# Attention products over 128 rows only, the second dilated group in whole segments of 256 keys, and rotary tables in each group's token order

## The chip, the cores and the metric

The kernel runs on one core of a Trainium2 chip. The metric is the device time of one execution in microseconds, median of several runs; smaller is better. Engines are named as the profile names them: PE is TensorE (its weight loads are PEld), DVE is VectorE, ACT is ScalarE, POOL is GpSimd, and SP is SyncE, whose queue issues most DMAs.

## The reference, cut to what matters

Two layers over 1024 tokens of 1024 channels. Each layer projects the normed input into four token mixers and their gates. The change lies in the third mixer, attention in three groups of four heads of 64 channels. Group 0 attends over neighbouring tokens, group 1 over every fourth and group 2 over every sixteenth, each within 64 places to either side:

```python
DILATED_CFG = ((128, 1), (512, 4), (2048, 16))
...
q = apply_rope(qkv[:, :, 0], cos, sin)
k = apply_rope(qkv[:, :, 1], cos, sin)
for g, (window, dil) in enumerate(DILATED_CFG):
    o, l = dilated_window_attention(q[:, :, g], k[:, :, g], v[:, :, g], dil, window // (2 * dil))
...
valid = (jnp.abs(qi - kj) <= half) & (kj >= 0) & (kj < L)
s = jnp.where(valid, s, NEG_BIG)
```

The group's order of tokens puts those of one residue side by side: one stretch of 1024 tokens in group 0, four of 256 in group 1, sixteen of 64 in group 2. Outputs of the groups are mixed by the softmax of their log-sum-exps.

## The kernel before, in words

Everything is float32, computed from pairs of shorter numbers: each operand is split into hi and lo (`split`: ACT copies hi, DVE subtracts lo), and a product takes three passes, hi by hi, hi by lo, lo by hi. Channels lie on partitions, tokens along the free axis, in halves of 512.

The main line of PE is one projection after another: `in_unit` loads 512 KB of weights, splits them and runs 24 products (L128, z) for each half of the tokens; `evac` empties the sum. Side work is written as generators in lanes; after every second group of passes `tick` lets each lane take a step, so that tiles of attention ("att"), taps of the convolution ("taps", 240 DVE instructions of L841), and the rest stand between the main products. The scheduler of the tile framework then fixes one order for each engine, and each engine works through its own in that order.

In each layer there are two pairs of heads, and for each pair the three groups. `att_group` runs the units of q, k and v of a group; then `att_tiles` of that group runs as side work during the units of the next.

`rope_unit` empties each half of a q or k unit. ACT copies the sums out of PSUM (rt, L365), four DMAs of 64 KB turn 32 rows at a time (rot, L367 and L368), three DVE instructions apply the tables, which lie in natural order of the tokens, and then come the split copies: these read rot in the group's order (a stride of 4 or 16 in groups 1 and 2) and write qa, qb, ka, kb in that order. A tile holds for head a hi above lo and for head b lo above hi. For q it is hi twice (L375, L377, four ACT copies), and lo of both heads in a third tile ql (L383 on ACT, L384 on DVE).

`products` makes the scores of two tiles of 128 queries: for each head one product over 128 rows (hi of q by hi and lo of k, L457) and one over 64 rows (lo of q by hi of k, L460), where those of the two heads use different halves of the array. `scores` adds the mask and takes the maximum on DVE, then the exponential on ACT (p, L474). `transposed` turns p on PE (pt, L486) and splits it; `weighted` multiplies by v (pv, L128) and ACT copies it out (o, L517). In groups 0 and 1 a tile's window begins 64 keys before it, so v lies in tiles of 64 rows at a segment's edges (veh, vel) and of 128 rows within it (vfh, vfl). A segment of group 1 has 256 keys and two tiles of queries, each with a window of 192 keys: one piece of 64 and one of 128.

Places for large tiles come from pools by tag: A has 11 (q, k and o among others), M has 11 (v's tiles, cos and sin among others).

Of the kernel before, what the change touches and what calls it, by code (L numbers as in the profile page):

```python
# [14 lines left out]
P = 128  # L15
# [23 lines left out]
# columns of the packed per-layer parameters  # L39
C_G, C_CW, C_CB, C_LG, C_LB, C_PS, C_BG, C_N = 0, 8, 70, 72, 74, 76, 78, 110  # L40
# columns of the packed constants
K_ID, K_M, K_M2, K_BC, K_BS, K_ED, K_IS, K_SG, K_O2, K_N = (
    0, 128, 384, 512, 640, 768, 800, 802, 804, 806)


class Net:
# [41 lines left out]
    def half_pair(self, name, tag):  # L88
        """hi and lo of one [P, H] operand."""
        t = self.slot(name, F32R, tag=tag)  # L90
        return t[:, 0:H], t[:, H:S]
# [10 lines left out]
    def split(self, hi, lo, src):  # L102
        """hi + lo = src exactly, each part with few enough bits for one pass."""
        self.nc.scalar.activation(out=hi, in_=src, func=AF.Copy)  # L104
        self.nc.vector.tensor_tensor(out=lo, in0=src, in1=hi.bitcast(F32), op=ALU.subtract)  # L105

    def load_unit(self, src, kc=KC, n=P, tag=None, ahead=AHEAD):
        """A right shape of weights: hi and lo."""
# [24 lines left out]
    def gemm(self, ps, w, x, hf, main=True):  # L133
        """x[k][hf]: hi and lo of the k-th 128 rows of the right operand, one half of the tokens."""
        self.passes(ps, [((w[0][:, k], w[1][:, k]), xk[hf]) for k, xk in enumerate(x)], main)

# [1 line left out]
    def setup(self):  # L138
# [4 lines left out]
        self.mask = c[:, K_M:K_M + 256]  # L143
# [9 lines left out]
    def load_constants(self):  # L153
        dma = self.nc.sync.dma_start
        dma(out=self.c, in_=self.a["consts"])
# [12 lines left out]
    def tok_stat(self, chunks, ones, name):  # L168
        """PSUM [token, 4 tiles, 2]: the mean over channels of the given [P, H] chunks' columns."""
# [24 lines left out]
    def spread(self, st, name):  # L194
        """[token, 4 tiles] to PSUM [P, H], the same in every partition."""
# [53 lines left out]
    def together(self, ws, xs, pss, ks=range(KC)):  # L249
        """Products that share their right operands."""  # L250
# [79 lines left out]
    def first_units(self, l, units):  # L330
        """Their first halves of the tokens before the second ones, whose norm is still under way."""
# [8 lines left out]
    def perm_dst(self, ap, g, hf):  # L340
        """Where the tokens of half hf lie in group g's order."""
# [4 lines left out]
        return ap.rearrange("p (r n) -> p r n", r=r)[:, :, hf * n:(hf + 1) * n]  # L346

# [5 lines left out]
    def rope_unit(self, l, u, g, cos, sin, q):  # L353
        """The rotated unit, split and stacked, for each of the two heads (a: rows 0:64, b: rows 64:128).
        For k: hi over lo (a), lo over hi (b). For q: hi twice (a, b), and lo, both heads."""
# [3 lines left out]
        xl = self.slot("ql", F32R) if q else None  # L359
        top, bot = slice(0, 64), slice(64, P)  # L360

        def evac(hf, ps):
            sl = slice(hf * H, hf * H + H)
            t, r = self.t2("rt"), self.t2("rot")
            nc.scalar.activation(out=t, in_=ps, func=AF.Copy)  # L365
# [3 lines left out]
            nc.vector.tensor_tensor(out=t, in0=t, in1=cos[:, sl], op=ALU.mult)  # L369
            nc.vector.tensor_tensor(out=r, in0=r, in1=sin[:, sl], op=ALU.mult)  # L370
            nc.vector.tensor_tensor(out=r, in0=r, in1=t, op=ALU.add)
            dst = lambda x, rows: self.perm_dst(x, g, hf)[rows]
            src = lambda rows: self.perm_src(r, g)[rows]
            for x, own, other in ((xa, top, bot), (xb, bot, top)):
                nc.scalar.activation(out=dst(x, own), in_=src(own), func=AF.Copy)  # L375
                if q:
                    nc.scalar.activation(out=dst(x, other), in_=src(own), func=AF.Copy)  # L377
                else:
                    nc.vector.tensor_tensor(out=dst(x, other), in0=src(own), in1=dst(x, own).bitcast(F32),
                                            op=ALU.subtract)  # L380
            if q:
                al = slice(0, P)
                nc.scalar.activation(out=dst(xl, al), in_=src(al), func=AF.Copy)  # L383
                nc.vector.tensor_tensor(out=dst(xl, al), in0=src(al), in1=dst(xl, al).bitcast(F32), op=ALU.subtract)  # L384
        self.in_unit(l, u, evac)
        return (xa, xb, xl) if q else (xa, xb)
# [9 lines left out]
    def v_tiles(self, vt, g, where):  # L396
        """v in the group's token order, tokens on partitions: hi, lo, rows by key offset."""
# [3 lines left out]
        if g == 2:  # L401
# [20 lines left out]
    def att_group(self, l, hp, g, cos, sin, done):  # L422
# [5 lines left out]
    def att_tiles(self, l, hp, g, q, k, vt, done):  # L428
# [7 lines left out]
        def window(t):  # L436
# [4 lines left out]
            a, b = max(base, q0 - 64), min(base + L, q0 + 192)  # L441
            m0 = a - (q0 - 64)
            return a, [a, q0 + 64], self.mask[:, m0:m0 + b - a]
# [3 lines left out]
        def products(t):  # L447
            # one bank per head: the two heads' products run in different rows of the array
            b = [self.aux("s0"), self.aux("s1")]
            s = {}  # L450
            for i in range(2):
# [4 lines left out]
                for h in range(2):  # L456
                    mm(s[i][h], q[h][:, qs], k[h][:, a:a + n], start=True, stop=False)  # L457
                for h in range(2):
                    r = slice(64 * h, 64 * h + 64)
# [805 lines left out]
```

## Time and profile before

| what | before |
|---|---|
| runs, median (lowest to highest) | 2097.05 us (2096.38 to 2097.84) |
| the profiled execution, span | 2096.5 us |
| PE busy | 2023.1 us (96%) |
| DVE busy | 1487.6 us (71%) |
| ACT busy | 1100.2 us (52%) |
| mean granted clock of PE | 0.985 |
| DMA, mean | 123 GB/s |

The page gives the profiled execution no time of its own beside the span. Busy time is an average over stages; PE is at or near full outside of the two attention stages (from about 110 to 450 us, and from 1170 to 1445 us). A row of the timeline reads: start in us, length in us, engine, line, operation, output<-input, shape, and in brackets how long the engine had stood idle and what ended that.

### The profile page before, as it was taken

What the parts mean: (1) busy time and instruction counts of PE and PEld (TensorE: products, weight loads), DVE (VectorE), ACT (ScalarE), POOL (GpSimd) and SP (SyncE); (2) the same over time, 40 slices, a digit from 0 to 9 for tenths busy, and PEclk for the clock granted to TensorE, in tenths of its full rate; (3) what the DMA queues carried; (4) which work ended last, traced back from release to release, by engine and by line L of the source; (5) the groups of instructions that cost most, each with busy time, mean ns of one, the idle gap of its engine ahead of it and who ended that gap; (6) DMA issues with size and microseconds to landing.
All of it is one profiled execution on the core that took longest, in us unless ns stands there. A gap on an engine that the chain in (4) does not pass through costs nothing.

```text
span 2096.5 us, 26763 instructions
## 1 busy us (share of the span) xinstructions
PE 2023.1 (96%) x9500; PEld 1645.9 (79%) x9500; DVE 1487.6 (71%) x2752; ACT 1100.2 (52%) x2025; POOL 41.3 (2%) x90
## 2 busy tenths in 40 slices
PE   8998898999999999999999998989999999999998
PEld 6776686778878888887888776867888888888888
DVE  7596777775657877877655867687555867777775
ACT  7347666657755433434321566666685744344451
POOL 0000000000000000000000000000000000000000
PEclk9999998999999999999999999999999999999999
DMA  6231122212586234236421321223127843243443
GB/s 229 81 106 58 49 82 62 96 41 81 190 284 235 86 136 141 100 112 245 158 85 49 106 65 52 77 71 101 46 87 266 278 159 125 97 141 131 144 167 101
DMA packets 122438, 257.81 MB, mean 123 GB/s; under 512 B 31808, under 2 KB 36544, under 8 KB 122304
## 3 DMA queue, kind: packets, MB, share of 16 engines
q1 hardware_dynamic: 111360, 216.25, 31.1%
q0 software_dynamic: 10944, 39.85, 5.6%
q8 instruction: 75, 1.23, 0.2%
q14 instruction: 59, 0.48, 0.1%
HBM read 176.16 MB, written 67.30 MB: 116 GB/s over the span
## 4 chain that ended last, share of the span: by engine, by line
PE 73%; DVE 10%; ACT 9%; DMA 4%; issue 3%; SPq 1%; DVEq 0%; ACTq 0%
PE z L128 20%; PE ga L128 12%; PE g L128 8%; PE gb L128 8%; PE py L128 8%; PE op L128 6%; PE z L255 3%; DVE cv L841 2%; PE pv L128 2%; PE pt L486 1%; ACT p L474 1%; DVE w L105 1%; ACT qa L377 1%; ACT ql L383 1%; ACT qb L375 1%
## 5 line engine op out<-in xcount | busy, mean ns | idle before, releaser
L128 PE MATMUL z<-h,w 128*128 128x512 f32 x3000 | 760.9, 404 | 1.4 <-DVE gp L604 1.4
L128 PEld LDWEIGHTS z<-h,w 128*128 128x128 f32 x3000 | 557.0, 192 | 119.5 <-DVE gp L604 1.8
L104 ACT ACTIVATE w<-wr 128x1024 fp32r<-128x1024 f32 (+1 forms) x135 | 137.8, 1022 | 185.9 <-PE z L128 80.2
L105 DVE TENSOR_TENSOR w<-wr,w 128x1024 fp32r<-128x1024 f32 (+1 forms) x135 | 158.9, 1179 | 97.8 <-ACT w L104 81.6
L128 PE MATMUL ga<-t,wf 128*128 128x512 f32 x768 | 188.9, 395 | 0.0
L128 PE MATMUL gb<-t,wf 128*128 128x512 f32 x768 | 187.4, 393 | 0.0
L128 PE MATMUL g<-h,wf 128*128 128x512 f32 x768 | 186.3, 391 | 0.0
L128 PE MATMUL op<-m,w 128*128 128x512 f32 (+1 forms) x960 | 181.3, 349 | 2.0 <-DVE m L105 1.9
L128 PE MATMUL py<-g,w 128*128 128x512 f32 x768 | 181.5, 395 | 0.5 <-ACT y L930 0.5
L841 DVE SCALAR_TENSOR_TENSOR cv<-cv,params 128x512 f32<-128x512 f32 x240 | 178.9, 745 | 2.2
L128 PEld LDWEIGHTS op<-m,w 128*128 128x128 f32 x960 | 153.6, 189 | 28.0 <-DVE m L105 3.5
L128 PEld LDWEIGHTS ga<-t,wf 128*128 128x128 f32 x768 | 144.3, 188 | 33.6
L128 PEld LDWEIGHTS py<-g,w 128*128 128x128 f32 x768 | 143.3, 188 | 34.3 <-ACT y L930 1.7
L128 PEld LDWEIGHTS gb<-t,wf 128*128 128x128 f32 x768 | 144.3, 188 | 32.9
L128 PEld LDWEIGHTS g<-h,wf 128*128 128x128 f32 x768 | 144.2, 188 | 31.9
L104 ACT ACTIVATE wf<-wr 128x512 fp32r<-128x512 f32 x144 | 90.9, 632 | 130.4 <-issue 48.4
L105 DVE TENSOR_TENSOR wf<-wr,wf 128x512 fp32r<-128x512 f32 x144 | 98.8, 686 | 21.5 <-ACT wf L104 20.3
L474 ACT ACTIVATE p<-p,nm 128x192 f32<-128x192 f32 (+2 forms) x192 | 84.4, 441 | 54.0 <-DVE nm L471 53.6
L105 DVE TENSOR_TENSOR pl<-pt,ph 128x256 fp32r<-128x256 f32 (+2 forms) x136 | 63.2, 465 | 54.1 <-ACT ph L104 53.8
L104 ACT ACTIVATE wf<-s 128x512 fp32r<-128x512 f32 x64 | 40.4, 632 | 107.3 <-PE gb L128 64.4
L128 PE MATMUL ga<-h,wf 128*128 128x512 f32 x384 | 93.5, 392 | 0.0
L128 PEld LDWEIGHTS ga<-h,wf 128*128 128x128 f32 x384 | 72.1, 188 | 16.4
(246 smaller groups left out, 2832.4 us busy)
## 6 DMA issues: line engine op xcount, KB each, us to landing
wr<-in_w_in_dram SPq DMA_DIRECT2D x75, 512.0 KB, 3.7
y<-y SPq DMA_DIRECT2D x128, 256.0 KB, 3.8
y<-y POOLq DMA_DIRECT2D x64, 512.0 KB, 4.8
wr<-in_w_gate_dram SPq DMA_DIRECT2D x48, 512.0 KB, 4.4
wr<-in_w_out_dram SPq DMA_DIRECT2D x32, 512.0 KB, 3.6
rot<-rt SPq DMA_DIRECT2D x192, 64.0 KB, 2.0
cv<-in_w_gate_dram SPq DMA_DIRECT2D x16, 512.0 KB, 5.1
wr<-in_w_branch_dram SPq DMA_DIRECT2D x16, 512.0 KB, 5.0
```

What stands on the lines that cost most here:

```text
L104: self.nc.scalar.activation(out=hi, in_=src, func=AF.Copy)
L105: self.nc.vector.tensor_tensor(out=lo, in0=src, in1=hi.bitcast(F32), op=ALU.subtract)
L128: self.nc.tensor.matmul(ps, w, x, start=(first and i + u == 0), stop=(i == n - 1 and u == 2), skip_group_check=open_)
L255: self.nc.tensor.matmul(ps, a[:, k], b, start=(k + j == 0), stop=(k == KC - 1 and j == 2))
L375: nc.scalar.activation(out=dst(x, own), in_=src(own), func=AF.Copy)
L377: nc.scalar.activation(out=dst(x, other), in_=src(own), func=AF.Copy)
L383: nc.scalar.activation(out=dst(xl, al), in_=src(al), func=AF.Copy)
L474: nc.scalar.activation(out=ph, in_=ph, func=AF.Exp, bias=nm[:, h:h + 1], accum_out=st[:, t, 2 + h:3 + h])
L486: nc.tensor.transpose(pt[:rows[ci], cs], p[:, off:off + rows[ci]], self.ident)
L841: self.tc.keep_in_program_order(nc.vector.scalar_tensor_tensor(out=y, in0=u[:, j:j + H], scalar=tap(j), in1=y, op0=ALU.mult, op1=ALU.add))
```

## The change

`rope_unit` now empties PSUM in the group's order at once: the ACT copy rt reads the sums with the stride and writes them side by side, and the DMAs, the tables and the split copies all work in that order. So the tables lie in DRAM three times, once for each group's order, and `att_group` loads cos and sin for each group of each head pair (24 loads of 512 KB in place of 4).

q is split like k: qa holds hi above lo, qb lo above hi (two ACT copies and two DVE subtractions per half). Once both halves are there, four DMAs of 256 KB copy the halves of the rows crosswise into two new tiles qt. `products` then takes for each head two products over all 128 rows: qa by ka gives hi by hi plus lo by lo, qt by ka gives the cross terms. lo by lo was not computed before. A group holds four tiles for q in place of three.

In group 1 every tile of queries now takes the whole segment of 256 keys, as two pieces of 128; the mask grows from 256 to 384 columns, and v is turned in eight tiles of 128 rows with none of 64. The Fourier basis (256 columns) leaves the constants and is loaded by `fourier_pq`.

```diff
     def rope_unit(self, l, u, g, cos, sin, q):
         xa, xb = self.slot(name + "a", F32R), self.slot(name + "b", F32R)
-        xl = self.slot("ql", F32R) if q else None
+        turned = [self.slot("qt", F32R) for _ in range(2)] if q else []
         def evac(hf, ps):
-            t, r = self.t2("rt"), self.t2("rot")
-            nc.scalar.activation(out=t, in_=ps, func=AF.Copy)
+            t, r, rc = self.t2("rt"), self.t2("rot"), self.t2("rc")
+            nc.scalar.activation(out=self.in_order(t, g), in_=self.perm_src(ps, g), func=AF.Copy)
...
-            src = lambda rows: self.perm_src(r, g)[rows]
+            src = lambda rows: self.in_order(r, g)[rows]
             for x, own, other in ((xa, top, bot), (xb, bot, top)):
                 nc.scalar.activation(out=dst(x, own), in_=src(own), func=AF.Copy)
-                if q:
-                    nc.scalar.activation(out=dst(x, other), in_=src(own), func=AF.Copy)
-                else:
-                    nc.vector.tensor_tensor(out=dst(x, other), in0=src(own), in1=dst(x, own).bitcast(F32),
-                                            op=ALU.subtract)
-            if q:
-                al = slice(0, P)
-                nc.scalar.activation(out=dst(xl, al), in_=src(al), func=AF.Copy)
-                nc.vector.tensor_tensor(out=dst(xl, al), in0=src(al), in1=dst(xl, al).bitcast(F32), op=ALU.subtract)
+                nc.vector.tensor_tensor(out=dst(x, other), in0=src(own), in1=dst(x, own).bitcast(F32),
+                                        op=ALU.subtract)
+            if hf == 1:
+                for x, y in zip((xa, xb), turned):
+                    for to, of in ((top, bot), (bot, top)):
+                        nc.sync.dma_start(out=y[to].bitcast(F32), in_=x[of].bitcast(F32))
         self.in_unit(l, u, evac)
-        return (xa, xb, xl) if q else (xa, xb)
+        return (xa, xb, *turned)

     def v_tiles(self, vt, g, where):
-        if g == 2:
+        if g:
             full = [j * P for j in range(8)]

+    def in_order(self, ap, g):
+        return ap if g == 0 else ap.rearrange("p (r n) -> p r n", r=4 if g == 1 else 16)

-    def att_group(self, l, hp, g, cos, sin, done):
+    def att_group(self, l, hp, g, done):
+        cos, sin = self.slot("cos", tag="M"), self.slot("sin", tag="M")
+        for i, t in enumerate((cos, sin)):
+            self.nc.sync.dma_start(out=t, in_=self.a["rope"][g, i])

         def window(t):
-            a, b = max(base, q0 - 64), min(base + L, q0 + 192)
-            m0 = a - (q0 - 64)
-            return a, [a, q0 + 64], self.mask[:, m0:m0 + b - a]
+            if g == 1:
+                a, b = base, base + L
+            else:
+                a, b = max(base, q0 - 64), min(base + L, q0 + 192)
+            m0 = a - q0 + P
+            return a, [a, a + P if g == 1 else q0 + 64], self.mask[:, m0:m0 + b - a]

         def products(t):
                 for h in range(2):
-                    mm(s[i][h], q[h][:, qs], k[h][:, a:a + n], start=True, stop=False)
-                for h in range(2):
-                    r = slice(64 * h, 64 * h + 64)
-                    mm(s[i][h], q[2][r, qs], k[h][r, a:a + n], start=False, stop=True)
+                    for j in (0, 2):
+                        mm(s[i][h], q[h + j][:, qs], k[h][:, a:a + n], start=(j == 0), stop=(j == 2))

     def fourier_pq(self, l, us, res):
+        bcs = self.t2("bcs")[:, 0:2 * P]
+        nc.sync.dma_start(out=bcs, in_=self.a["consts"][:, K_BC:K_ALL])

 def _constants():
+    rope = np.stack([rope.reshape(2, P, 2, H // r, r).transpose(0, 1, 2, 4, 3).reshape(2, P, S) for r in (1, 4, 16)])
```

How the instructions stand now is shown at three places in the first layer's first head pair, where group 1's tiles run beside group 2's units. On PE, the first pair of score tiles of group 1 (s0 and s1 are the sums of the two heads); before:

```order
L457 MATMUL s0_1876<-ka_1341,qa_1196 128x192
L457 MATMUL s1_1877<-kb_1342,qb_1197 128x192
L460 MATMUL s0_1876<-ka_1341,ql_1198 128x192
L460 MATMUL s1_1877<-kb_1342,ql_1198 128x192
L457 MATMUL s0_1876<-ka_1341,qa_1196 128x192
L457 MATMUL s1_1877<-kb_1342,qb_1197 128x192
L460 MATMUL s0_1876<-ka_1341,ql_1198 128x192
L460 MATMUL s1_1877<-kb_1342,ql_1198 128x192
```

and of the change:

```order
L465 MATMUL s0_1881<-ka_1353,qa_1205 128x256
L465 MATMUL s0_1881<-ka_1353,qt_1207 128x256
L465 MATMUL s1_1882<-kb_1354,qb_1206 128x256
L465 MATMUL s1_1882<-kb_1354,qt_1208 128x256
L465 MATMUL s0_1881<-ka_1353,qa_1205 128x256
L465 MATMUL s0_1881<-ka_1353,qt_1207 128x256
L465 MATMUL s1_1882<-kb_1354,qb_1206 128x256
L465 MATMUL s1_1882<-kb_1354,qt_1208 128x256
```

The eight products stay eight; those with ql, over 64 rows, are replaced by products with qt over 128 rows, a head's two follow each other, and the columns go from 192 to 256.

On ACT, the second half of group 2's q unit (rot_1813 before, rot_1831 now) and the first exponentials of group 1 (p with st1); before:

```order
L375 ACTIVATE qa_1682<-rot_1813 64x16x32
L377 ACTIVATE qa_1682<-rot_1813 64x16x32
L375 ACTIVATE qb_1683<-rot_1813 64x16x32
L377 ACTIVATE qb_1683<-rot_1813 64x16x32
L383 ACTIVATE ql_1684<-rot_1813 128x16x32
L365 ACTIVATE rt_1906<-z_1836 128x512
L474 ACTIVATE p_1886,st1_1875<-p_1886,nm_1887 128x192 x2
L474 ACTIVATE p_1893,st1_1875<-p_1893,nm_1894 128x192 x2
```

and of the change:

```order
L370 ACTIVATE rt_1918<-z_1857 128x512
L380 ACTIVATE qa_1700<-rot_1831 64x16x32
L380 ACTIVATE qb_1701<-rot_1831 64x16x32
L479 ACTIVATE p_1891,st1_1880<-p_1891,nm_1892 128x256 x2
L479 ACTIVATE p_1898,st1_1880<-p_1898,nm_1899 128x256 x2
```

Two copies stand ahead of the exponentials where five stood, and k's copy out of PSUM has moved ahead of both.

On SP's queue, the rotations of group 2's q (second half, rot_1831) and k (rot_1919, rot_1995) in the changed kernel:

```order
L373 DMA rot_1831<-rt_1830 32x512
L372 DMA rot_1919<-rt_1918 32x512
L386 DMA qt_1702<-qa_1700 64x1024 x2
L386 DMA qt_1703<-qb_1701 64x1024 x2
L373 DMA rot_1919<-rt_1918 32x512
L372 DMA rot_1919<-rt_1918 32x512
L373 DMA rot_1919<-rt_1918 32x512
L372 DMA rot_1995<-rt_1994 32x512
L373 DMA rot_1995<-rt_1994 32x512
L372 DMA rot_1995<-rt_1994 32x512
L373 DMA rot_1995<-rt_1994 32x512
L427 DMA cos_2185<-in_rope_dram 128x1024
```

The four copies into qt stand within the rotation of k's first half, each waiting for qa or qb to be written; before, nothing stood between q's rotations and k's but a weight load. The next group's tables follow, and wait until earlier tiles of v give up their places.

In ACT's order the first write of kb now waits, in nine of the ten groups that follow another in their layer, for the last score products of the group before, whose q or k tile had its place; before, only the copies qb and ql of one group in each layer waited for such products.

More of the change, by code (lines that the diff above doesn't have):

```diff
@@ L40 @@
 C_G, C_CW, C_CB, C_LG, C_LB, C_PS, C_BG, C_N = 0, 8, 70, 72, 74, 76, 78, 110
-K_ID, K_M, K_M2, K_BC, K_BS, K_ED, K_IS, K_SG, K_O2, K_N = (
-    0, 128, 384, 512, 640, 768, 800, 802, 804, 806)
+K_ID, K_M, K_M2, K_ED, K_IS, K_SG, K_O2, K_N, K_BC, K_BS, K_ALL = (
+    0, 128, 512, 640, 672, 674, 676, 678, 678, 806, 934)
 class Net:
@@ L142, in setup @@
         self.ident = c[:, K_ID:K_ID + P]
-        self.mask = c[:, K_M:K_M + 256]
+        self.mask = c[:, K_M:K_M + 384]
         self.mask2 = c[:, K_M2:K_M2 + P]
@@ L154, in load_constants @@
         dma = self.nc.sync.dma_start
-        dma(out=self.c, in_=self.a["consts"])
+        dma(out=self.c, in_=self.a["consts"][:, 0:K_N])
         dma(out=self.fg, in_=self.a["final_g"])
@@ L368, in evac @@
                 nc.sync.dma_start(out=r[b + 32:b + 64], in_=t[b:b + 32])
-            nc.vector.tensor_tensor(out=t, in0=t, in1=cos[:, sl], op=ALU.mult)
+            nc.vector.tensor_tensor(out=rc, in0=t, in1=cos[:, sl], op=ALU.mult)
             nc.vector.tensor_tensor(out=r, in0=r, in1=sin[:, sl], op=ALU.mult)
-            nc.vector.tensor_tensor(out=r, in0=r, in1=t, op=ALU.add)
+            nc.vector.tensor_tensor(out=r, in0=r, in1=rc, op=ALU.add)
             dst = lambda x, rows: self.perm_dst(x, g, hf)[rows]
-            src = lambda rows: self.perm_src(r, g)[rows]
+            src = lambda rows: self.in_order(r, g)[rows]
             for x, own, other in ((xa, top, bot), (xb, bot, top)):
                 nc.scalar.activation(out=dst(x, own), in_=src(own), func=AF.Copy)
-                if q:
-                    nc.scalar.activation(out=dst(x, other), in_=src(own), func=AF.Copy)
-                else:
-                    nc.vector.tensor_tensor(out=dst(x, other), in0=src(own), in1=dst(x, own).bitcast(F32),
-                                            op=ALU.subtract)
-            if q:
-                al = slice(0, P)
-                nc.scalar.activation(out=dst(xl, al), in_=src(al), func=AF.Copy)
-                nc.vector.tensor_tensor(out=dst(xl, al), in0=src(al), in1=dst(xl, al).bitcast(F32), op=ALU.subtract)
+                nc.vector.tensor_tensor(out=dst(x, other), in0=src(own), in1=dst(x, own).bitcast(F32),
[4 more added lines that the diff above has]
+                        nc.sync.dma_start(out=y[to].bitcast(F32), in_=x[of].bitcast(F32))
         self.in_unit(l, u, evac)
-        return (xa, xb, xl) if q else (xa, xb)
+        return (xa, xb, *turned)
     def v_unit(self, l, u, g):
@@ L733, in fourier_pq @@
             ps = self.aux("gcp")
-            for i, col in enumerate((K_BC, K_BS)):
-                nc.tensor.matmul(ps[:, i * 256:i * 256 + 256], self.c[:, col:col + P], wf[:, c], start=True, stop=True)
+            for i in range(2):
+                nc.tensor.matmul(ps[:, i * 256:i * 256 + 256], bcs[:, i * P:i * P + P], wf[:, c], start=True, stop=True)
             nc.scalar.activation(out=gc[:, c * H:c * H + H], in_=ps, func=AF.Copy)
@@ L1129, in layer @@
         pool = self.pool(l)
-        cos, sin = self.slot("cos", tag="M"), self.slot("sin", tag="M")
-        nc.sync.dma_start(out=cos, in_=self.a["rope"][0])
-        nc.sync.dma_start(out=sin, in_=self.a["rope"][1])
         att = self.dr.tile([2, P, S], F32, name=f"att{l}")
@@ L1136, in layer @@
             for g in range(3):
-                self.att_group(l, hp, g, cos, sin, done)
+                self.att_group(l, hp, g, done)
             self.start("mix", self.att_mix(done, att[hp]))
@@ L1182, in _constants @@
     f = np.float32
-    c = np.zeros((P, K_N), f)
+    c = np.zeros((P, K_ALL), f)
     c[:, K_ID:K_ID + P] = np.eye(P, dtype=f)
-    p, i = np.arange(P)[:, None], np.arange(256)[None, :]
-    c[:, K_M:K_M + 256] = np.where((i >= p) & (i <= p + P), 0.0, NEG)
+    p, i = np.arange(P)[:, None], np.arange(-64, 320)[None, :]
+    c[:, K_M:K_M + 384] = np.where((i >= p) & (i <= p + P), 0.0, NEG)
     c[:, K_M2:K_M2 + P] = np.where(p // 64 == np.arange(P)[None, :] // 64, 0.0, NEG)
```

## The prediction

> **What bounds the kernel now.** I read the page first, then busy time by stretch, then the waits of PE, then two places in the timeline.
>
> ```profile
> span 2096.5 us, 26763 instructions
> ```
>
> The sum below is made against this span of the profiled execution; the median of the three runs, 2097.05 us, lies 0.5 us above it, and that half microsecond is added at the end. Busy time by stretch, for the two stretches in which the attention units and most of the attention tiles run (columns: stretch, its length, busy us of PE, weight loads, DVE, ACT, POOL with instruction counts, granted clock, DMA share, GB/s):
>
> ```profile
> 110.00:450.00 340.00, 314.08 (x1496) 249.57 (x1495) 258.51 (x567) 211.05 (x450) 0.00 (x0) 0.95 0.24 72
> 1170.00:1445.00 275.00, 251.18 (x1228) 201.03 (x1228) 205.72 (x450) 180.05 (x374) 0.00 (x0) 0.96 0.24 71
> ```
>
> PE is the bound, but it stands still 340 - 314.08 = 25.9 us and 275 - 251.18 = 23.8 us, together **49.7 us**, and its clock is granted at 0.95 and 0.96, which costs 0.05 x 340 + 0.04 x 275 = **28 us** more. Whom PE waits for (us in total, times, longest):
>
> ```profile
> PE pt L486 <- ACT p L474: 23.5, 6, 7.3
> PE s L457 <- ACT o L517: 8.6, 3, 4.1
> PE pv L128 <- ACT ph L104: 8.3, 5, 2.6
> ```
>
> These 14 waits hold 40.4 us, and ACT ends every one. What ACT does meanwhile, at one of the longest (its rows in order, then the PE row that waits):
>
> ```profile
> 227.34 1.12 ACT L375 ACTIVATE qa<-rot 64x512 fp32r<-64x512 f32 x1 [5.22 <-DVE rot L371]
> ...
> 231.71 1.05 ACT L383 ACTIVATE ql<-rot 128x512 fp32r<-128x512 f32 x1
> ...
> 233.98 0.45 ACT L474 ACTIVATE p<-p,nm 128x192 f32<-128x192 f32 x1 [0.73 <-DVE nm L471]
> ```
> ```profile
> 234.58 1.29 PE L486 MATMUL pt<-consts,p 128*64 128x128 f32 x4 [5.59 <-ACT p L474]
> ```
>
> From 227.34 to 232.76 ACT writes the five split copies of one half of a q unit, for the next group; the exponential that the present group's transposes need stands behind them in the same queue. The clock falls after such a wait:
>
> ```profile
> 229.00:236.00 7.00, 1.40 (x5) 1.11 (x6) 3.89 (x22) 6.23 (x14) 0.00 (x0) 0.84 0.11 28
> 236.00:243.00 7.00, 7.00 (x26) 5.46 (x24) 4.83 (x7) 5.92 (x15) 0.00 (x0) 0.68 0.40 110
> ```
>
> PE is full again in the second stretch, but at 0.68 of its clock.
>
> **ACT's part of the change.** The price of a split copy depends on how it reads (min/median/max ns):
>
> ```profile
> L375 ACT ACTIVATE qa<-rot x24: 612/1108/1150, 124.3 to 1428.5; 64x512 fp32r<-64x512 f32 x24
> ```
> ```profile
> L379 DVE TENSOR_TENSOR ka<-rot,ka x24: 684/1030/1074, 138.4 to 1447.1; 64x512 fp32r<-64x512 f32 x24
> ```
> ```profile
> L392 ACT ACTIVATE vt<-z x24: 577/597/602, 136.0 to 1448.6; 128x512 f32<-128x512 f32 x24
> ```
>
> The least, 0.61 us, is group 0, whose order is the natural one; 1.1 us is the two dilated groups, which read rot with a stride of 4 or 16. The v unit writes the same places in the groups' order and reads its sums in PSUM with that stride, and it takes 0.6 us in every group: neither the write in pieces nor the strided read of PSUM costs anything. The change moves the reordering into that read, and all later work reads in order. Per half of a q unit in a dilated group ACT pays 5 x 1.1 = 5.5 us now and 2 x 0.62 = 1.2 us after (two copies; the other two and ql go): 4.3 us less. Group 0 pays 3.1 and then 1.2. Per half of a k unit it is 2.2 and then 1.2. With 16 dilated and 8 natural halves of each kind ACT loses 16 x 4.3 + 8 x 1.9 + 16 x 1.0 = 100 us of work. DVE gives up 24 ql subtractions (16 at 1.05, 8 at 0.68: 22 us) and the strided part of 32 k subtractions (32 x 0.35 = 11 us), and gains 48 q subtractions (48 x 0.68 = 33 us): nothing on balance.
>
> What this is worth is what PE waits. Of the 40.4 us, each wait behind a q block can shrink by at most 4.3 us. The longest, 7.3 us, ends behind k copies,
>
> ```profile
> 1385.92 1.12 ACT L375 ACTIVATE ka<-rot 64x512 fp32r<-64x512 f32 x1 [4.63 <-DVE rot L371]
> ```
>
> and shrinks by some 2 us (four copies by 0.5); the 5.59 keeps 1.3, and I allow one more of that kind. That leaves some 8 of 40.4, so at most 32 us go. DVE, which is relieved of nothing, will be late next, and I give 4 us back to it: **-28 us**. The bounds are 0 and -49.7. The clock's 28 us follow the waits; 28/49.7 of them is 16, and a little more because the long waits go first: **-17 us**, between 0 and -28. [...]
>
> **PE's part.** A pair of score tiles with 256 keys now (first start, the two half-row products, start of what follows):
>
> ```profile
> 168.41 0.28 PE L457 MATMUL s<-ka,qa 128*128 128x256 f32 x1
> ...
> 168.74 0.38 PE L460 MATMUL s<-ka,ql 64*128 64x256 f32 x1
> 168.75 0.38 PE L460 MATMUL s<-kb,ql 64*128 64x256 f32 x1
> ...
> 169.80 0.74 PE L128 MATMUL z<-h,w 128*128 128x512 f32 x2
> ```
>
> The two products of 64 rows start 0.01 us apart, so they do run beside each other; but the pair takes 169.80 - 168.41 = 1.39 us for eight products. With 128 keys (group 2):
>
> ```profile
> 286.53 0.22 PE L457 MATMUL s<-ka,qa 128*128 128x128 f32 x1
> ...
> 287.68 5.78 PE L128 MATMUL z<-h,w 128*128 128x512 f32 x24
> ```
>
> 1.15 us. And what six products of 256 columns cost, first all of 128 rows, then three of 128 and three of 64:
>
> ```profile
> 204.99 0.28 PE L128 MATMUL pv<-ph,vfh 128*128 128x256 f32 x1
> ...
> 205.69 2.91 PE L128 MATMUL z<-h,w 128*128 128x512 f32 x12
> 208.44 0.28 PE L128 MATMUL pv<-ph,vfh 128*128 128x256 f32 x1
> ...
> 209.45 0.50 PE L128 MATMUL z<-h,w 128*128 128x512 f32 x1
> ```
>
> Six in a row of 128 rows take 0.70 us, 0.117 each; the mixed six take 1.01 us. So eight score products of 128 rows should take 8 x 0.117 = 0.94 us at 256 columns. At 128 columns they cannot take more than that, nor less than half; I take 0.8. There are 16 pairs in each of the three groups (two head pairs, two layers, four pairs a unit). Group 0: 16 x 0.45 = 7 us. Group 1 goes from 192 keys (taken midway, 1.27) to 256 at 0.94: 16 x 0.33 = 5 us. Group 2: 16 x 0.35 = 6 us. The 32 weighted sums of group 1 become unmixed: 32 x 0.31 = 10 us, and 16 transposes of v go, under 2 us. That is 29 us on the engine that sets the end; while it waits for ACT a shorter product only lengthens the wait, and it still does so for part of a tenth of the stage, so I take **-27 us**. Bounds: group 2 between 0.21 and 0.68 a pair gives -25 to -34. [...]
>
> **What is added.** Wider tiles in group 1 (64 exponentials from 192 to 256 keys, and as many masked maxima on DVE):
>
> ```profile
> L474 ACT ACTIVATE p<-p,nm x192: 384/440/514, 163.1 to 1554.2; 128x192 f32<-128x192 f32 x80, 128x128 f32<-128x128 f32 x64, 128x256 f32<-128x256 f32 x48
> ```
>
> At most 514 - 440 = 74 ns each, 5 us of ACT in all and by the same count about as much of DVE (an estimate), largely paid back by one split of 512 columns in place of two of 256. The 48 copies into qt (256 KB each) and 20 more loads of rotary tables go through SP's queue. Issue and landing, by the nearest rows:
>
> ```profile
> L367 SPq DMA_DIRECT2D rot<-rt x96: 507/581/2572, 114.8 to 1437.5; - x96
> ```
> ```profile
> y<-y SPq DMA_DIRECT2D x128, 256.0 KB, 3.8
> ```
>
> Four issues of 0.58 us and a landing of 3.8 are 6.1 us. The q block shown above ends at 232.76 and its scores begin at 286.53, so 54 us cover them: cost nothing. Behind the four stand most of the rotations of k's two halves, the next tables and a weight load; if the copies had to wait there, at most 2.3 us of issue would move into k's chain, whose result has the same cover. For the whole, DMA at a share of 0.24 has room. The two small loads of the Fourier basis lie beside the load of w_fourier that is waited for anyway.
>
> Sum: 2096.5 - 28 - 17 - 27 = 2024.5, with the half microsecond **2025 us**.
>
> **The rivals.** (A) As forecast, 1996 to 2050: chance 0.64. The lower end is nearly all of 49.7 + 28 + 29; the upper one is PE's part with 20 us of waits and clock.
>
> (B) DVE takes ACT's place. For and against, DVE beside PE in two stretches:
>
> ```profile
> 140.00:160.00 20.00, 20.00 (x97) 15.92 (x96) 17.82 (x34) 9.75 (x13) 0.00 (x0) 1.00 0.18 52
> ```
> ```profile
> 1380.00:1400.00 20.00, 12.71 (x53) 9.81 (x52) 19.30 (x46) 9.98 (x25) 0.00 (x0) 0.74 0.06 19
> ```
>
> In the first DVE is busy 17.82 of 20 us while PE is full, in the second 19.30 and PE starves. With 258.5 us of DVE work in a stage cut from 340 to 300 it would be at 0.86. If it then ends most waits anew, a third of waits and clock is saved (26 us) and two thirds of PE's part is seen (18): 2053. Range 2045 to 2068, chance 0.19.
>
> (C) The 64-row products were worth their switch: four full products a tile cost one more than two full ones and one shared slot, 0.117 x 96 tiles = 11 us, in place of the 18 us gained. 2025 + 29 = 2054. Chance 0.03, since 1.39 us a pair is already more than eight times 0.117. [...]
>
> (D) The change doesn't do what it says: if writing q and k in pieces were the dear part, the copies would stay at 1.1 us, ACT would lose 3.3 of 5.5 us a block and DVE would gain 22 us (32 more subtractions at 1.03 and 16 at 0.68, less ql's 22). Waits and clock give 30 instead of 45, less 10 for DVE: 2050. The v row speaks against it. Chance 0.04.
>
> (E) Slower. Slots of tag A are 11; a group now holds qa, qb, two qt, ka, kb and o (seven, six before), so two groups in flight want 13 with the next o still to come. In nine of the ten groups that follow another, the first write of kb now waits for the last score products of the group before, and ACT's queue stands behind it. If each of the nine holds PE for 5.6 us, as the wait shown, and costs another 3.4 us of clock (28 of 49.7, as above, and a little), 81 us come back: 2106. It decides from 72/9 = 8 us a boundary. Against it: the exponentials of the earlier tiles stand ahead of kb in ACT's order, and what PE does up to those products needs nothing behind it. Chance 0.07.
>
> (F) Gains and losses cancel within 0.2%, about what a measurement of this kernel can tell from no change: 0.03.
>
> **How the numbers follow.** A alone leaves out 0.36; with B the range of 1996 to 2068 holds over 0.8. Faster by over 0.2% are A to D, 0.90; the same 0.03; slower 0.07.
>
> **What would show it.** Right: qa and ka copies at 0.62 us in all groups, eight score products in under 1.0 us, the waits of PE for p under 10 us in place of 23.5, the clock near 0.98 in both stretches. Wrong: q's rows still at 1.1 us (D), a score pair above 1.3 us (C), DVE as the releaser of most waits (B), or kb's copy on ACT idle before PE's products (E).

## The result and the profile after

The changed kernel takes **2004.73 us** (median of 4 runs, 2004.13 to 2007.35) against 2097.45 us beside it: ratio 0.9557, 95% interval 0.954 to 0.9573. Run again in the last set of experiments it gave 2006.59 us, ratio 0.9567 (0.9554 to 0.958). The forecast was 2025 us, in a range of 1996 to 2068; the time is 20 us below the forecast and inside the range. One execution of a later kernel, u_prod, took 6916 us in place of some 2020 for a reason that the record doesn't show; its ratio leaves that execution out.

The page of the changed kernel (span, then busy time by engine):

```profile
span 2005.6 us, 26782 instructions
...
PE 1967.1 (98%) x9484; PEld 1625.6 (81%) x9484; DVE 1486.6 (74%) x2740; ACT 1000.5 (50%) x1917; POOL 41.1 (2%) x90
```

PE stands still for 2005.6 - 1967.1 = 38.5 us of the whole span, where it was 2096.5 - 2023.1 = 73.4. ACT has lost 99.7 us of work, as worked out (100); DVE has lost 1. The two attention stretches, with the columns of before:

```profile
110.00:450.00 340.00, 330.88 (x1756) 277.44 (x1755) 287.17 (x629) 191.81 (x460) 0.00 (x0) 1.00 0.40 117
1170.00:1445.00 275.00, 272.16 (x1485) 230.09 (x1483) 221.59 (x522) 168.69 (x412) 0.00 (x0) 1.00 0.38 112
```

PE stands still 9.1 and 2.8 us there (25.9 and 23.8 before), and the clock is whole. The stages end earlier now, so the same stretches of time hold more work: DVE is busy 287.17 of 340 us, at 0.84, beside a PE that is nearly full. The waits of PE (total, times, longest):

```profile
PE z L255 <- ACT cv L271: 7.4, 1, 7.4
...
PE pv L128 <- DVE pl L105: 2.2, 3, 0.9
...
PE pt L491 <- DVE nm L476: 1.6, 1, 1.6
...
PE pt L491 <- ACT o L522: 0.8, 2, 0.5
```

The largest one stands at the kernel's start (PE's first product begins at 7.41 us), before any attention. The waits for p on ACT, 23.5 us before, have gone. The copies (min/median/max ns, first and last start):

```profile
L370 ACT ACTIVATE rt<-z x48: 571/597/601, 111.1 to 1363.0; 128x512 f32<-128x512 f32 x48
```
```profile
L380 ACT ACTIVATE qa<-rot x24: 618/632/635, 123.1 to 1351.3; 64x512 fp32r<-64x512 f32 x24
...
L380 ACT ACTIVATE ka<-rot x24: 616/632/635, 136.9 to 1371.7; 64x512 fp32r<-64x512 f32 x24
...
  PE s L465: 6.5, 5
...
  PEld pt L491: 2.0, 1
```
```profile
L381 DVE TENSOR_TENSOR qa<-rot,qa x24: 684/685/689, 123.8 to 1352.8; 64x512 fp32r<-64x512 f32 x24
```

The strided read has moved into rt, whose 48 copies take 571 to 601 ns in every group: there it costs nothing. The copies behind it take 0.62 to 0.64 us in every group. The two indented rows tell who kept ACT waiting before these copies, and who waited for them: ACT did stand behind the last score products of the group before (rival E), five times, 6.5 us in all, but PE's weight load waited for it only once, 2.0 us. Eight score products now, first at 256 columns, then the last four of a pair at 128 columns (first start, last product, what follows):

```profile
206.99 0.28 PE L465 MATMUL s<-ka,qa 128*128 128x256 f32 x1
...
207.82 0.28 PE L465 MATMUL s<-kb,qt 128*128 128x256 f32 x1
...
207.94 5.67 PE L128 MATMUL z<-h,w 128*128 128x512 f32 x24
```
```profile
284.06 0.28 PE L465 MATMUL s<-ka,qa 128*128 128x128 f32 x1
...
284.40 0.27 PE L465 MATMUL s<-kb,qt 128*128 128x128 f32 x1
284.51 1.60 PE L128 MATMUL z<-h,w 128*128 128x512 f32 x6
```

207.94 - 206.99 = 0.95 us for eight (1.39 before; 0.94 was forecast), and 284.51 - 284.06 = 0.45 us for four at 128 columns, 0.90 for eight (1.15 before; 0.8 was forecast): half the columns save next to nothing.

**The span in three parts.** For each profiled execution, "still" is the span less PE's busy time, "clock" is half of the time that PE worked at half clock, and "work" is the rest of its busy time, what PE would need at full clock (clock and work to about 0.3 us):

| kernel | span | still | clock | work |
|---|---|---|---|---|
| before | 2096.5 | 73.4 | 22.4 | 2000.7 |
| changed | 2005.6 | 38.5 | 0.0 | 1967.1 |
| difference | -90.9 | -34.9 | -22.4 | -33.6 |

The medians differ by 92.7 us, a little more than the spans, since the profiled execution of the changed kernel was the slowest of its four.

### The profile page after: what moved, and what is told of

It reads as the page before. It is cut to its first block, busy times and chain, and to the rows that moved or that the text cites. A ratio compares the mean times of both kernels' runs of the same rounds, so it can differ in the third digit from the quotient of the medians.

```text
span 2005.6 us, 26782 instructions
## 1 busy us (share of the span) xinstructions
PE 1967.1 (98%) x9484; PEld 1625.6 (81%) x9484; DVE 1486.6 (74%) x2740; ACT 1000.5 (50%) x1917; POOL 41.1 (2%) x90
## 4 chain that ended last, share of the span: by engine, by line
PE 82%; DVE 9%; ACT 4%; DMA 3%; issue 2%; SPq 0%; DVEq 0%; ACTq 0%
PE z L128 25%; PE ga L128 13%; PE g L128 9%; PE op L128 8%; PE gb L128 8%; PE py L128 8%; PE z L255 3%; DVE cv L848 2%; PE pv L128 2%; PE s L465 1%; PE pt L491 1%; DVE w L105 1%; DMA mt<-m 1%; ACT o L522 1%; DVE p L474 1%
## 5 line engine op out<-in xcount | busy, mean ns | idle before, releaser
L128 PE MATMUL z<-h,w 128*128 128x512 f32 x3000 | 744.3, 397 | 2.5 <-DVE gp L609 1.4
L128 PEld LDWEIGHTS z<-h,w 128*128 128x128 f32 x3000 | 546.7, 188 | 111.4 <-DVE gp L609 1.8
L104 ACT ACTIVATE wf<-wr 128x512 fp32r<-128x512 f32 x144 | 90.9, 631 | 131.7 <-issue 48.3
L479 ACT ACTIVATE p<-p,nm 128x256 f32<-128x256 f32 (+2 forms) x192 | 87.9, 459 | 42.9 <-DVE nm L476 42.5
L522 ACT ACTIVATE o<-pv 64x128 f32<-64x128 f32 x192 | 67.6, 352 | 48.6 <-PE pv L128 46.7
```

Of the source, the lines that this page charges most:

```text
L128: self.nc.tensor.matmul(ps, w, x, start=(first and i + u == 0), stop=(i == n - 1 and u == 2), skip_group_check=open_)
L479: nc.scalar.activation(out=ph, in_=ph, func=AF.Exp, bias=nm[:, h:h + 1], accum_out=st[:, t, 2 + h:3 + h])
L522: nc.scalar.activation(out=dst, in_=src, func=AF.Copy)
```

## The experiments

Three parts can be undone or made alone: the token order (PSUM read in the group's order, tables and split copies in order), the score products (q split like k, qt by DMA, 128 rows), and the whole segments of group 1. The span's three parts are given for each (still / clock / work), with the median and its ratio to the kernel before.

**act4s: ACT's q block as long as before.**

```diff
+            if q:
+                for own in (top, bot, top, bot):
+                    nc.scalar.activation(out=self.in_order(t, g)[own], in_=self.perm_src(r, g)[own], func=AF.Copy)
```

> The changed kernel with four more ACT copies of 64x512 in each half of a q unit (read with the group's stride, written into rt, which nobody reads any more). In the dilated groups ACT's q block is then 2 x 0.62 + 4 x 1.1 = 5.6 us, as long as before the change (5.5); PE's products, the tables and group 1's segments stay as changed. Theory 'length of ACT's block': PE's waits behind the block and the half-clock phases come back, 40 us of waits and up to 28 us of clock, 2004.7 + 50 to 68 = 2055 to 2073 us. Rival 'order': the waits went because k's copy out of PSUM and the exponentials now stand elsewhere in ACT's queue, or because DVE reads in order; then the longer block costs under 10 us, 2005 to 2015 us.

Measured: 2043.17 us, 0.9736 (0.9719 to 0.9752); 58.8 / 15.4 / 1970.9. The added copies took 1.10 us in the median. 38 us came back, below the 50 to 68 of the first theory and far over the 10 of the rival. Who waited:

```profile
PE pv L128 <- ACT ph L104: 11.6, 7, 2.8
...
PE pt L494 <- ACT p L482: 6.5, 9, 3.5
PE pt L494 <- ACT o L525: 5.1, 4, 2.1
```

The time ACT spends there matters, but a block of the old length gives back 20 of the 35 us of standing still and 15 of the 22 of clock, not all. Nothing waits for the added copies themselves, while in the kernel before DVE waited for ql, the last of the block; whether that makes the rest, this run doesn't tell.

**u_order: token order undone**, with the tables in natural order, loaded once a layer.

```diff
-            nc.scalar.activation(out=self.in_order(t, g), in_=self.perm_src(ps, g), func=AF.Copy)
+            nc.scalar.activation(out=t, in_=ps, func=AF.Copy)
...
-            src = lambda rows: self.in_order(r, g)[rows]
+            src = lambda rows: self.perm_src(r, g)[rows]
...
```

> The changed kernel with the token order undone: PSUM is read in natural order, tables in natural order loaded once a layer, and the split copies read rot with a stride of 4 or 16 again. ACT's q block is 2 x 1.1 = 2.2 us and its k block 2.2 us (1.2 each in the changed kernel), DVE gets 64 x 0.35 = 22 us more. Theory 'length of ACT's block': 2.2 us is still short of the 5.5 us that made the long waits, so little comes back: 5 to 15 us, 2010 to 2020 us, and no or one half-clock phase. Rival 'the order is the gain' (strided reads by ACT and DVE together made the waits): half of the waits and of the clock come back, 2035 to 2050 us.

Measured: 2033.13 us, 0.9687 (0.9672 to 0.9702); 54.4 / 6.7 / 1970.7. The theory of the block's length failed: a q block of 2.2 us, far from the old 5.5, still brings back 16 us of standing still and two fifths of that in clock. The rival's 2035 to 2050 was nearer.

**u_prod: score products undone**, five ACT copies in order, products of 128 and 64 rows.

```diff
...
-                    for j in (0, 2):
-                        mm(s[i][h], q[h + j][:, qs], k[h][:, a:a + n], start=(j == 0), stop=(j == 2))
+                    mm(s[i][h], q[h][:, qs], k[h][:, a:a + n], start=True, stop=False)
+                for h in range(2):
+                    r = slice(64 * h, 64 * h + 64)
+                    mm(s[i][h], q[2][r, qs], k[h][r, a:a + n], start=False, stop=True)
```

> The changed kernel with the score products undone: q hi twice and lo in a third tile, five ACT copies per half (5 x 0.62 = 3.1 us, in order), products over 128 and 64 rows mixed; token order and group 1's segments as changed. Theory 'length of ACT's block and price of the mixed products': PE's products cost 0.45 a pair more in groups 0 and 1 and 0.35 in group 2, 16 x (0.45 + 0.45 + 0.35) = 20 us, and the block of 3.1 us brings back a quarter of the waits and clock, 10 to 20 us: 2034 to 2045 us. Rival 'the products cost what they cost only while PE is the bound': waits come back whole and hide the products, 2050 to 2065 us. Rival 'sharing was worth it': 2005 to 2015 us.

Measured: 2020.36 us, 0.9625 (0.9608 to 0.9642); 31.3 / 3.5 / 1983.5. PE's work rises by 16.4 us (the score products alone by 20.0, as worked out), but hardly a wait comes back (2.8 us for p, in two places), although ACT's q block is 3.1 us: PE even stands still 7 us less, perhaps because slower products give ACT more time. All three expectations missed; the first one by the waits it wanted back.

**u_seg: group 1's windows of 192 keys back.**

```diff
...
-            if g == 1:
-                a, b = base, base + L
-            else:
-                a, b = max(base, q0 - 64), min(base + L, q0 + 192)
+            a, b = max(base, q0 - 64), min(base + L, q0 + 192)
...
```

> The changed kernel with group 1's windows of 192 keys in pieces of 64 and 128 back; the rest as changed. Theory: 32 weighted sums become mixed again (32 x 0.31 = 10 us), 16 transposes of v come back (2 us), the scores lose 64 columns (about -2 us): 2013 to 2017 us, seen whole since PE is full. Rival 'hidden': PE's own work in group 1 lies beside waits, under 4 us: 2005 to 2008 us.

Measured: 2021.77 us, 0.9633 (0.9618 to 0.9648); 36.6 / 1.8 / 1981.6. Work rises by 14.5 us: the weighted sums by 9.7, the transposes of p by 2.4 and of v by 1.5. That is seen whole, and a little more: the time lies 5 us above the range expected, in which the transposes of p had no place and the narrower scores were to give 2 us back (they gave 0.4).

**act_order: token order undone and three strided ACT copies more**, with PE's changed products. ACT is then busy for about as long as before (1095.7 us, 1100.2 before), but DVE for 25 us longer (1512.8 us, 1487.6 before), since the split of q by two subtractions stays and now reads with the stride.

```diff
...
+            if q:
+                for own in (top, bot, top):
+                    nc.scalar.activation(out=self.in_order(t, g)[own], in_=src(own), func=AF.Copy)
...
```

> Token order undone and three more ACT copies of 64x512 per half of a q unit, read with the group's stride: ACT's q block is 5 x 1.1 = 5.5 us and its k block 2.2 us, DVE reads with the stride, all as before the change; PE's products and group 1's segments are the changed ones. Theory 'lengths on ACT and DVE are the whole cause of the waits and of the clock': PE's idle time comes back to some 70 us in all (38.8 in the changed kernel, 73.7 before) and the half-clock loss to 15 to 22 us, 2004.7 + 50 to 62 = 2055 to 2067 us. Rival 'the two lengthenings lie behind one another': no worse than the longer block alone (2043), 2040 to 2050 us. Rival 'they add': 2004.7 + 38.4 + 28.4 = 2072 us or more.

Measured: 2068.28 us, 0.9857 (0.9837 to 0.9878); 76.9 / 22.0 / 1968.2. Standing still and clock are those of before (73.4 and 22.4) to within 4 us, and the work is that of the changed kernel. So the 33 us of work are those of PE's products, and ACT and DVE together can account for all of the 57 us of waits and clock; how much of it DVE's 25 us more bring, the run doesn't tell. The time lies 1 us over the first theory's range and 4 below the sum of the two undone alone, so it doesn't tell whether they add.

**only_order, only_prod, only_seg: one part alone**, on the kernel before.

> The kernel before with the token order alone: reading PSUM in the group's order, tables in that order, split copies in order; q in three tiles with five ACT copies (5 x 0.62 = 3.1 us), mixed products and windows of 192 keys as before. Theory: the order alone takes most of the waits and of the clock (it is the run with the score products undone, 2020.4, plus the 17 us that group 1's segments are worth there): 2033 to 2042 us. Rival 'parts add': undoing the order cost 28.4 us, so doing it alone gains 28: 2065 to 2072 us.

> The kernel before with the 128-row score products alone (q split like k, qt by DMA): ACT's q block is 2 x 1.1 = 2.2 us, k's block 2.2; natural order, strided split copies and windows of 192 keys as before. Theory: PE's products gain 19 us and the shorter block takes half or more of the waits and the clock (the run with the order undone, 2033.1, plus 14 to 17 for group 1's segments): 2045 to 2052 us. Rival 'parts add': undoing the products cost 15.6, so 2079 to 2084 us.

> The kernel before with group 1's whole segments of 256 keys alone; all else as before (five strided ACT copies a q half, mixed score products). Theory: 14 us of PE's work go (32 weighted sums and 16 transposes unmixed), and part is eaten by the waits that stay: 2082 to 2090 us, idle time at 70 us or more. Rival 'hidden': PE waits that much longer, 2094 to 2098 us.

| kernel | us | ratio | still | clock | work |
|---|---|---|---|---|---|
| only_order | 2039.45 | 0.9726 (0.9711 to 0.974) | 35.0 | 5.0 | 1999.9 |
| only_prod | 2046.45 | 0.9757 (0.9741 to 0.9773) | 52.7 | 10.0 | 1984.5 |
| only_seg | 2076.17 | 0.9901 (0.9886 to 0.9915) | 65.2 | 22.3 | 1987.7 |

The order and the products came out as their theories said; the segments gained 6 us more than expected, and PE stood still for 65 us, not for 70 or more. The order alone, with five ACT copies a block, takes all the standing still that the whole change takes, and PE's work stays as it was. The products alone take 21 us of standing still, half of the clock's loss and 16 of work. The parts alone gain 58, 51 and 21 us, some 130 in all; the whole gains 93. What they share is waits and clock, which can go only once; the work adds (0.8 + 16.2 + 13.0 = 30.0, of 33.6).

**pad_act and pad_dve: what the strided reads cost, on one engine at a time, as more copies.**

```diff
+                if g:
+                    nc.scalar.activation(out=t[own, 0:320], in_=r[own, 0:320], func=AF.Copy)
```
```diff
+                if g:
+                    nc.vector.tensor_tensor(out=t[other, 0:240], in0=r[own, 0:240], in1=r[own, 0:240],
+                                            op=ALU.subtract)
```

> The changed kernel, and behind every split copy of the dilated groups (two per half, q and k) one more ACT copy of 64x320 into rt, which nobody reads any more: ACT's share of what the strided reads cost (1.1 in place of 0.62 us a copy, some 0.45 us each, 64 copies, 29 us), with DVE left as changed. Undoing the token order on ACT and DVE together cost 28.4 us. Theory 'the order is worth what ACT gains': 2018 to 2030 us, PE waiting for p and o of ACT. Rival 'it is DVE's part': under 8 us, 2005 to 2012 us. Of the clock, every stretch at half rate should follow a piece of 3.4 us in which PE stood for half of it or more (1.7 us), as in the nine traces so far.

> The changed kernel, and behind every split subtraction of the dilated groups one more DVE subtraction of 64x240 into rt, which nobody reads any more: DVE's share of what the strided reads cost (some 0.35 us each, 64 of them, 22 us), with ACT left as changed. It also tries the rival of the prediction that DVE, at 0.84 of the first stretch, is late next. Theory 'ACT': DVE has room, under 8 us, 2005 to 2012 us. Rival 'DVE': 2018 to 2030 us, with DVE as the releaser of PE's new waits.

Measured: pad_act 2003.97 us, 0.9556 (0.9543 to 0.9569), 35.7 / 1.8 / 1965.9, the copies at 455 ns; pad_dve 2008.56 us, 0.9577 (0.9564 to 0.959), 36.3 / 0.0 / 1967.7, the subtractions at 402 ns. Neither costs more than 2 us beside the changed kernel of the same set (2006.59), though the one lengthens ACT's copies toward what they take in u_order and the other does so for DVE's subtractions. By busy time pad_act adds 22 us to ACT, where u_order adds 30, and pad_dve 21 us to DVE, where u_order adds 23. The first theory missed for ACT and held for DVE. Three readings of one place tell more: group 2's first q half beside group 1's second pair of tiles, in u_order, in the changed kernel and in pad_act (line numbers differ by a few between kernels).

```profile
213.94 0.28 PE L462 MATMUL s<-ka,qa 128*128 128x256 f32 x1
...
215.83 1.12 ACT L380 ACTIVATE qa<-rot 64x512 fp32r<-64x512 f32 x1 [3.83 <-DVE rot L376]
...
216.97 1.06 ACT L380 ACTIVATE qb<-rot 64x512 fp32r<-64x512 f32 x1
...
218.06 0.51 ACT L476 ACTIVATE p<-p,nm 128x256 f32<-128x256 f32 x1
...
218.71 0.33 PE L488 MATMUL pt<-consts,p 128*128 128x128 f32 x1 [1.84 <-ACT p L476]
```
```profile
213.45 0.28 PE L465 MATMUL s<-ka,qa 128*128 128x256 f32 x1
...
214.18 0.63 ACT L380 ACTIVATE qa<-rot 64x512 fp32r<-64x512 f32 x1 [2.68 <-DVE rot L376]
...
214.40 2.01 PE L128 MATMUL z<-h,w 128*128 128x512 f32 x8
214.83 0.63 ACT L380 ACTIVATE qb<-rot 64x512 fp32r<-64x512 f32 x1
215.49 0.51 ACT L479 ACTIVATE p<-p,nm 128x256 f32<-128x256 f32 x1
...
216.25 0.27 PE L491 MATMUL pt<-consts,p 128*128 128x128 f32 x1
```
```profile
213.70 0.51 ACT L481 ACTIVATE p<-p,nm 128x256 f32<-128x256 f32 x1 [2.31 <-DVE nm L478]
...
214.70 0.62 ACT L380 ACTIVATE qa<-rot 64x512 fp32r<-64x512 f32 x1
```

In u_order and in the changed kernel p stands behind qa and qb, and PE has the same eight products (2.0 us) to do meanwhile. In the changed kernel that is just enough. In u_order qa starts 1.89 us after the pair's first score product (213.94) and not 0.73 after it (213.45), and the two copies take 0.92 us longer: 2.08 us late, of which 1.84 is PE's wait. In pad_act p stands ahead of qa: the scheduler has put the block elsewhere. The order is not made with the lengths of strided copies: with the four copies of act4s reading in order, all engines' instructions stand in the same order, row by row. That suggests what sets the pads apart: a length that the plan knows is planned around, the 0.48 us that a stride adds is not, and PE, whose cover is cut as close as the 2.0 us above, pays for it. It is argued, not shown: the four copies in order were not run, nor were both pads together, and u_order lengthens both engines where each pad lengthens one.

**g0_full and after2: whole pieces of 128 keys in group 0 too.**

```diff
...
-            if g == 1:
-                a, b = base, base + L
-            else:
-                a, b = max(base, q0 - 64), min(base + L, q0 + 192)
+            a = min(max(base, q0 - 64), base + L - 256)
-            return a, [a, a + P if g == 1 else q0 + 64], self.mask[:, m0:m0 + b - a]
+            return a, [a, a + P], self.mask[:, m0:m0 + 256]
...
-                edge += [base, base + L - 64]
+                edge += [base, base + P, base + L - 256, base + L - P]
-        for offs, rows, nm in ((full, P, "vf"), (edge, 64, "ve")):
+        for offs, rows, nm in ((full, P, "vf"), (edge, P, "ve")):
```

> The changed kernel with group 0's first and last tile of queries also on whole pieces of 128 keys (windows of 256 keys held inside the segment; four more tiles of v of 128 rows in place of two of 64). Theory 'a mixed product costs PE its price wherever it stands': eight weighted sums lose 0.31 us each (2.5 us) and the 64-row transposes of p and v go (1 to 2 us), less 1 us for more columns: 2.5 to 3.5 us faster than the changed kernel, 2001 to 2003 us. Rival 'too few to be seen, or eaten by wider splits on ACT and DVE': 2004 to 2007 us.

> The changed kernel again, beside the three others: 2004 to 2007 us, so that a gain of 2.5 us by whole pieces in group 0 is told against runs of the same call.

Measured: 1999.3 us (1998.41 to 2000.63), 0.9535 (0.9522 to 0.9548), beside 2006.59 us (2005.88 to 2006.71) for the changed kernel: 7 us faster, more than expected. Work is 2.7 us less (1965.4 for 1968.1), in sum as the price of the mixed products had it, though the weighted sums give 1.8 of it in place of 2.5; the rest is standing still (31.8 for 36.7), which had not been forecast and was not taken apart. This is the fastest version here.

## Why the prediction was right, and where its sizes were off

**Direction and stage: right.** PE was the bound, the gain lies in the two attention stretches, and it came from standing still, clock and work, the three terms of the sum. All three were mis-sized the same way, so no error hid another:

| term | forecast | measured |
|---|---|---|
| PE's waits | -28 | -34.9 |
| clock | -17 | -22.4 |
| PE's products | -27 | -33.6 |

**Waits.** The prediction left 8 us of the 40.4 behind the longest blocks and gave 4 back to DVE. Neither came: no wait for p, and none for anything above 1.6 us, is left in the attention stretches, and DVE at 0.84 makes PE wait 2.2 us for pl. pad_dve adds 21 us of busy time to DVE and costs 2 us at most, so DVE had room (rival B). The step that carried the term, "each wait behind a q block can shrink by at most 4.3 us", gave nearly the right size by a reason that holds only in part, so the near hit is partly luck. By it the length of ACT's block would decide. But the blocks of 3.1 us in only_order and u_prod leave PE still for 35.0 and 31.3 us, no more than the changed kernel, while the block of 2.2 us with strided reads in u_order leaves 54.4. In all 14 traces, every kernel in which ACT and DVE read rot in order stands still for 31 to 39 us, and every one in which one of them reads it with a stride for 52 to 77. act_order shows that ACT and DVE can account for the whole; why a strided read costs more than as much added work is not shown.

The step also stopped at the last releaser of each wait. Behind it stands DVE. At the wait that the prediction shows, DVE stood 2.73 us for ql, the last of the five copies, and nm, which p needs, came only behind ql's subtraction. Before the wait of 7.3 us, ACT itself stood 2.51 us for nm:

```profile
232.79 1.01 DVE L384 TENSOR_TENSOR ql<-rot,ql 128x512 fp32r<-128x512 f32 x1 [2.73 <-ACT ql L383]
...
233.72 0.16 DVE L471 TENSOR_SCALAR nm<-st 128x2 f32<-128x2 f32 x1
```
```profile
1391.79 0.45 ACT L474 ACTIVATE p<-p,nm 128x192 f32<-128x192 f32 x1 [2.51 <-DVE nm L471]
```

In the kernel before, DVE stood for ql 32.7 and 35.9 us in the two attention stretches. The change has no ql, so DVE, "which is relieved of nothing" in the prediction, kept its work but lost this waiting. That fits the room that it had; no run takes it alone, and only_order, whose DVE still waits 24.9 us for ql there, stands still no longer than the changed kernel.

**Clock.** The prediction's 28 us count all time at half clock in the two stretches, also that in which PE stood still; by the measure of the table, 22.4 us were lost before the change. And the share of the long waits was the wrong measure: the loss went to nothing, not by three fifths. The last section has the reason.

**Products.** By PE's work, start to next start at full clock:

| product | before | changed | forecast |
|---|---|---|---|
| scores s | 63.4 | 44.5 | -18 |
| weighted sums pv | 73.1 | 62.8 | -10 |
| transposes of v and p | 39.0 | 36.7 | under -2 |
| main products z | 776.8 | 772.3 | none |

The prices read from the pairs and from the mixed six held (-18.9, -10.3, -2.3). The deduction of 2 us for products that only lengthen a wait was wrong, since hardly a wait was left, and the 4.5 us at z were not foreseen; PE's other products grew by 2.4 us together. Kernels without mixed products outside of group 0 have 771.8 to 774.1 us at z, those with some of them 773.7 to 775.7, and only_order, with all, 777.0. The ranges overlap, so that mixed products cost the main products beside them anything is a guess, and what makes the mixed six 0.31 us longer is not shown either. Sharing the array was worth nothing here (rival C): u_prod brings the 64-row pairs back and its score products cost 20.0 us more. The others: copies at 0.63 us, not 1.1 (D); ACT did stand at kb, 6.5 us in five places, at a price of 2.0 us on PE's weight loads and not 81 (E). The added work cost nothing that shows: qt's issues took 0.50 and 0.56 us, DMA's share rose from 0.24 to 0.40.

## What to carry to other kernels

Reorder where the read is free: the same strides cost ACT 0.48 us a copy when it reads rot and nothing that shows when it empties PSUM (571 to 601 ns), and the engine that pays need not be the bound to set the time. A mixed set of row tilings on PE had a price here (1.01 us for the mixed six, 0.70 for six of one kind), so one tiling that computes more (unused keys, a low-by-low product) can be the shorter one; try that in every place, as group 0 shows. And add up parts by their own resource: PE's work adds, waits and clock that several parts remove count once. And follow a wait past its last releaser: that engine may itself have stood behind another.

## What the runs showed of the hardware

In these traces the clock changes in pieces of 3.41 us, on a grid that runs through the whole execution: in every trace with more than one stretch at half clock, all begin a whole number of 3.413 us apart (in the kernel before, those from 185.90, 233.69 and 332.68 us on lie 14 and 29 pieces apart), and all but the one that runs to the end last 1 to 4 pieces. Two traces cut at this grid, before and u_order (columns as in the stretches above; the clock stands third from the end):

```profile
226.86:230.28 3.42, 2.12 (x10) 1.31 (x9) 3.20 (x10) 2.92 (x3) 0.00 (x0) 1.00 0.00 0
230.28:233.69 3.41, 0.00 (x0) 0.00 (x0) 0.90 (x1) 2.94 (x4) 0.00 (x0) 1.00 0.00 0
233.69:237.10 3.41, 2.50 (x8) 1.92 (x9) 1.94 (x15) 3.12 (x11) 0.00 (x0) 0.50 0.36 78
237.10:240.52 3.42, 3.42 (x10) 2.65 (x9) 3.26 (x5) 2.39 (x11) 0.00 (x0) 0.50 0.07 6
```
```profile
216.21:219.62 3.41, 1.57 (x9) 0.86 (x9) 3.32 (x7) 3.04 (x7) 0.00 (x0) 1.00 0.45 99
219.62:223.03 3.41, 3.41 (x11) 2.63 (x10) 3.21 (x12) 3.33 (x10) 0.00 (x0) 0.50 0.96 222
```

In the first, PE stands 1.30 us of a piece and the next one is still at full clock; then it stands a whole piece, and the next two are at half. In the second, the piece behind one wait of 1.84 us is at half. Over all 14 traces, the first 6 us of each aside, of the pieces at full clock in which PE stood for 1.8 us or more, 55 of 55 were followed by one at half clock; of those with 1.2 to 1.8 us, 7 of 61; with less, 0 of 8087. So in these runs waits of under 1.2 us in a piece cost themselves alone, and after 1.8 us or more the next piece ran at half clock, which costs up to 1.7 us of work (half of the 3.41). Between the two either happened (in the kernel before, the piece from 162.01 us, in which PE stood for 1.69 us, was followed by full clock, and the one from 349.74, with 1.76 us, by half): three of the seven stood for 1.5 to 1.6 us, less than the 1.7 us named in what was expected of pad_act. That is why the whole 22.4 us returned when the longest wait, the start and the end aside, fell to 1.7 us, with some luck: one piece of the changed kernel stood for 1.69 us and cost nothing more.

The other thing is the stride's price. With the strides of 4 and 16 numbers that the two dilated groups have, a copy of 64x512 out of rot takes 1.12 and 1.10 us on ACT in the kernel before, and 0.63 in natural order; a subtraction of that size takes 1.06 and 1.03 us on DVE, and 0.69 in natural order. No run tries another stride, and what makes the strided read longer is not shown. ACT's read of PSUM at the same strides takes 571 to 601 ns in the changed kernel, and 575 to 602 ns in natural order before.
